# A decoder layer on one core: the branch of the top-k selection asked for directly behind its searches, two query projections queued behind its flag, and the selection masks built one behind the other

## The chip, the core and the metric

The kernel runs on one core of one Trainium2 chip. A core has five engines that run side by side, each through its own list of instructions in order: PE (TensorE, matrix products and transposes), DVE (VectorE), ACT (ScalarE), POOL (GpSimd) and SP (here only a queue that starts DMA transfers). An engine waits for another by a semaphore. The metric is device time in microseconds (us) of one execution, and what is compared is the median of several runs. Matrix products here are 128 rows deep and write up to 512 columns into a PSUM bank.

## The reference

One layer of a hybrid decoder trunk on 1024 positions of 1024 channels. The part that matters here is the sparse attention: an indexer scores every earlier position for each query position, the 256 best are selected, and eight query heads attend to those alone.

```python
score = einsum('bth,bths->bts', w, relu(dots))          # the indexer, 128 query rows at a time
score = where(causal, score, -inf)
_, idx = top_k(score, 256)                              # 256 keys for each of the 1024 queries
kg, vg = k[idx], v[idx]                                 # two kv heads, eight query heads
logits = einsum('btkgd,btjkd->btkgj', qg, kg) * 64**-0.5
p = softmax(where(sel_ok, logits, -inf)); o = einsum('btkgj,btjkd->btkgd', p, vg)
```

The rest of the layer (adaptive norms, a spatial gating unit, output projection, and a feed-forward block of 4096 channels) stands around it and is not touched.

## The kernel before

The 1024 positions are cut into 8 blocks of 128 query rows, numbered 0 to 7; block b has 128(b+1) causal keys. Blocks 0 and 1 have no more than 256 keys, so nothing is selected there, and their mask is the causal one alone. For blocks 2 to 7 the kernel does not gather: it finds for each row the value of the 256th score and turns the scores into an additive mask `BI` (0 for a selected key, a huge negative number for others).

- **Search** (`select`, L602 to L628): for each block a bitwise search, on DVE (L585, L587, L589) or on ACT (L597), for the upper 16 bits of the threshold, then a shortcut for the lower 16 bits that works as long as at most 8 keys share the upper bits.
- **Branch** (`search_rest`, L630 to L642): DVE counts in `more` the blocks in which the shortcut did not do (L632), PE sums this over the partitions with a 1x1 product (L634, the *flag*), DVE turns the sum into an integer `rest` (L635), reads it into a register (L637) and branches (L638) over a second search of the lower bits. The branch stands in a critical section: the program is cut there into blocks of instructions, every engine has a jump to its next block at that place, and DVE waits in front of its own jump for what the other engines have ahead of theirs.
- **Mask** (`mask(b)`, L644 to L660): three instructions on one column (L648, L649, L651) build the threshold `tf`; then over the row of scores L654 (below the threshold, with a count), L655 (equal to it), L656 (a running sum of the equal ones), two one-column instructions (L657, L658), L659 (which equal ones are too many) and L660 (the mask into `BI`).
- **Query projections** (`q_proj`, L542 to L547): 24 products of 512 columns for a block (`proj`, L296 to L302), a copy by ACT (L546), the rotary embedding on POOL.
- **Attention** in 32 units (L689), four for each block, in the block order 0, 7, 1, 6, 5, 4, 3, 2. For each pair of units `q_stack` makes the left operand (transposes on PE, L319, a copy on ACT, L379, and the rest of its high and low split on DVE, L380). A unit takes the products with the keys (L704), adds `BI` and takes the maximum on DVE (L705), the exponential on ACT (L708), then transposes (L743), copies (L724) and products with the values (L729).

The order on each engine is made by a scheduler from priorities: a smaller number goes first, and `stage(n)` sets the counter to 100000 n. Searches have numbers from 400000 on, the q projections stand in stage 4, and attention in stage 6. `after(ins, prev)` (L82) asks that one instruction stand behind another in the order, without a semaphore. In the program before, `search_rest()` and `mask(7)` are called in the loop over units, at u == 3, and the other masks behind units 4, 6, 8, 9 and 10 (L801); the scheduler may pull a mask ahead, and it does.

Of the kernel before, what the change touches and what calls it, by code (L numbers as in the profile page):

```python
# [16 lines left out]
OP = mybir.AluOpType  # L17
# [11 lines left out]
BIG = float(2.0 ** 100)  # L29
# [8 lines left out]
def trunk(ctx, tc, x, c, positions, w_ada, b_ada, g_pre_mix, w_in, g_sgu_v, w_spatial, b_spatial,  # L38
          g_out_sgu, g_out_attn, w_out, g_post_mix, g_pre_ffn, w_ff1, w_ff2, g_post_ffn, out):
    nc = tc.nc  # L40
    V, A, G, T = nc.vector, nc.scalar, nc.gpsimd, nc.tensor
# [5 lines left out]
    def nm(s):  # L47
        uid[0] += 1
        return f"{s}_{uid[0]}"
# [32 lines left out]
    def after(ins, prev):  # L82
        if prev is not None:
            tc.add_manual_dep(ins.ins, prev.ins.name,
                              mybir.DependencyInfo(mybir.DependencyClass.NoSync, mybir.DependencyReason.DATA),
                              reason="in this order")
# [4 lines left out]
    ones = ct([P, 1], F32, "ones")  # L91
# [45 lines left out]
    for k in range(KD):  # L137
        load_ada(0, (k,))
        if k:
            dst, src, off, n = small.pop()  # L140
            nc.sync.dma_start(dst, rows(src, off, n))
    for i in range(4):
        load_x(i)
        if small:
            dst, src, off, n = small.pop()
# [149 lines left out]

    def proj(p, j, wt, n, ks=range(KD)):  # L296
        h, t = hT[j // 4], (j % 4) * P
        for k in ks:
            lh, ll = h[:, 0, k, t:t + P], h[:, 1, k, t:t + P]
            T.matmul(p[:, :n], lh, wt[k][:, 0, :n], start=k == 0, stop=False)  # L300
            T.matmul(p[:, :n], lh, wt[k][:, 1, :n], start=False, stop=False)  # L301
            T.matmul(p[:, :n], ll, wt[k][:, 0, :n], start=False, stop=k == KD - 1)  # L302

    def rope(t, j, nh, pool):

# [40 lines left out]
    for j in range(NB):  # L346
# [4 lines left out]
        if j < 4:  # L351
            p = p1[j]
            proj(p, j, wC1, 328, range(4, KD))
        else:
            p = p_mm()
# [172 lines left out]
    for cc in range(2):  # L528
        wt = w_chunk(w_in, [(0, C_U + 256 * cc, 256), (256, C_V + 256 * cc, 256)])
        for j in range(NB):  # L530
            p = p_mm()
# [6 lines left out]
    wQ = w_chunk(w_in, [(0, C_Q, 512)])  # L538
    QT = {}
    OB = (0, 7, 1, 6, 5, 4, 3, 2)  # L540

    def q_proj(b):  # L542
        p = p_mm()
        proj(p, b, wQ, 512)
        QT[b] = qp.tile([P, 512], F32, tag="q", name=nm("q"), bufs=8)
        A.activation(QT[b], p, AF.Copy)  # L546
        rope(QT[b], b, 8, qp)  # L547

    for b in OB:
        q_proj(b)  # L550
        if pend:
            last_gelu = gating(*pend.pop(0))
# [14 lines left out]
    more = ct([P, 7], F32, "more")  # L567
# [62 lines left out]
    def search_rest():  # L630

        V.tensor_scalar(more[:, :6], KDS, 8.0, None, op0=OP.is_gt, op1=OP.add, accum_out=more[:, 6:7])  # L632
        p = p_tr()
        T.matmul(p[:1, :1], more[:, 6:7], ones, start=True, stop=True)  # L634
        V.tensor_copy(rest, p[:1, :1])  # L635
        with tc.tile_critical():
            r = V.value_load(rest)  # L637
            with V.If(r > 0):  # L638
                for b in range(2, NB):
                    cnt, sg, kk, tf, kq, lf, top8, kd, th, lo, hi = ST[b]  # L640
                    search(BI[:, boff[b]:boff[b] + P * (b + 1)].bitcast(U16), 15, lf, cnt, kd, kk, V.drain)
                V.drain()  # L642

    def mask(b):  # L644
        n = P * (b + 1)
        cnt, sg, kk, tf, kq, lf, top8, kd, th, lo, hi = ST[b]
        sc = score(b)
        V.tensor_copy(lo, lf)  # L648
        V.scalar_tensor_tensor(th, hi, 16, lo, op0=OP.logical_shift_left, op1=OP.bitwise_or)  # L649

        V.tensor_tensor(tf, th.bitcast(F32), sg, op=OP.mult)  # L651
        lt = BI[:, boff[b]:boff[b] + n]
        eq = up.tile([P, 1024], BF, tag="uv", name=nm("eq"), bufs=2)[:, :n]
        V.tensor_scalar(lt, sc, tf, None, op0=OP.is_lt, op1=OP.add, accum_out=cnt)  # L654
        V.tensor_scalar(eq, sc, tf, BIG, op0=OP.is_equal, op1=OP.mult)  # L655
        V.tensor_tensor_scan(sc, eq, eq, 0.0, op0=OP.add, op1=OP.max)  # L656
        V.tensor_scalar(cnt, cnt, float(TOPK - n), BIG, op0=OP.add, op1=OP.mult)  # L657
        V.tensor_tensor(cnt, cnt, sc[:, n - 1:n], op=OP.add)  # L658
        V.scalar_tensor_tensor(eq, sc, cnt, eq, op0=OP.is_gt, op1=OP.mult)  # L659
        V.scalar_tensor_tensor(lt, lt, -BIG, eq, op0=OP.mult, op1=OP.subtract)  # L660

    for b, pri in PRI:
        tc.cur_priority = pri
        select(b)


    stage(6)
# [135 lines left out]
    logits(0)  # L803
    stack_for(2)
    for u, (b, grp, pair) in enumerate(units):
        if u == 3:
            search_rest()
            mask(7)
        if u + 1 < len(units):
            logits(u + 1)  # L810
        values(u)
        if u in MASKS:
            mask(MASKS[u])
        if u == 12:
            u_stack.close()
            sc_stack.close()
            o_stack, op_ = push("op")
        stack_for(u + 3)
        if u % 4 == 2:
            finish_a(b)  # L820
        if u in (24, 28):
            ada_use(u // 4 - 4)
        if u in (20, 24, 28):
            ADA[u // 4 - 3] = ada_sum(u // 4 - 3)
        if u % 4 == 0 and u:
            finish(OB[u // 4 - 1])
        if u == 14:
            WO[0] = w_chunk(w_out, [(0, 0, 512)], gout, tile_of=wo_tile)
        if u >= 19 and u % 2:
            oproj0(OB[(u - 19) // 2])  # L830
# [71 lines left out]
    for j in range(NB):  # L902
# [4 lines left out]
        p = p_mm()  # L907
# [358 lines left out]
```

## Time and profile before

| what | before |
|---|---|
| median of 3 runs | 1272.2 us (1265.81 to 1272.71) |
| profiled execution, its own time | 1273.95 us |
| span of its instructions | 1272.2 us |
| PE busy in the span | 92% |
| DVE, ACT, POOL busy | 70%, 51%, 16% |
| mean granted TensorE clock | 0.959 of full |

Over the whole span PE is the engine that is always busy, so what matters is where it is not. The page cuts the span into 40 slices of 31.8 us and gives the busy tenths of each engine and the granted clock; the slices in which PE shows a low digit are the place to look at. Below that, three views are used: the busy times of each engine in chosen stretches, the list of who waited for whom, and the list of instructions in order of time. In the last one a row has the start in us, the duration in us, the engine, the line, the operation, out<-in, the shape, how many were merged, and in brackets the idle time before it and what ended it.

### The profile page before, as it was taken

What the parts mean: (1) busy time and instruction counts of PE and PEld (TensorE: products, weight loads), DVE (VectorE), ACT (ScalarE), POOL (GpSimd) and SP (SyncE); (2) the same over time, 40 slices, a digit from 0 to 9 for tenths busy, and PEclk for the clock granted to TensorE, in tenths of its full rate; (3) what the DMA queues carried; (4) which work ended last, traced back from release to release, by engine and by line L of the source; (5) the groups of instructions that cost most, each with busy time, mean ns of one, the idle gap of its engine ahead of it and who ended that gap; (6) DMA issues with size and microseconds to landing.
All of it is one profiled execution on the core that took longest, in us unless ns stands there. A gap on an engine that the chain in (4) does not pass through costs nothing.

```text
span 1272.2 us, 16825 instructions
## 1 busy us (share of the span) xinstructions
PE 1171.3 (92%) x5785; PEld 987.3 (78%) x5785; DVE 891.8 (70%) x1894; ACT 644.5 (51%) x1306; POOL 206.8 (16%) x280
## 2 busy tenths in 40 slices
PE   4889888889749999999889999999999899999997
PEld 4877677668639999878767878888888788888886
DVE  6833999987297656646898776556537846776668
ACT  4544557452327855545634555555544454445442
POOL 3675614132200000003630000000000000000001
PEclk9899999899759999989979999999999999999999
DMA  9420202010002124436404854344359355633335
GB/s 336 147 79 30 71 13 83 13 50 13 10 0 59 34 88 176 179 106 242 163 33 147 284 165 159 135 154 164 133 195 373 121 167 172 215 100 100 99 89 210
DMA packets 80240, 162.42 MB, mean 128 GB/s; under 512 B 7724, under 2 KB 32920, under 8 KB 80152
## 3 DMA queue, kind: packets, MB, share of 16 engines
q1 hardware_dynamic: 80136, 161.33, 37.7%
q8 instruction: 45, 0.74, 0.2%
q14 instruction: 43, 0.35, 0.1%
q10 hardware_dynamic: 16, 0.00, 0.0%
HBM read 119.36 MB, written 41.94 MB: 127 GB/s over the span
## 4 chain that ended last, share of the span: by engine, by line
PE 51%; DVE 12%; issue 4%; DMA 3%; ACT 1%; POOL 1%; SPq 0%; DVEq 0%; POOLq 0%; ACTq 0%
PE tr L1146 8%; PE lg L1146 8%; PE mm L1146 5%; PE mm L729 3%; PE lg L963 2%; PE lg L964 2%; PE lg L965 2%; DVE w L853 2%; PE tr L963 2%; PE tr L964 2%; PE tr L965 2%; PE tr L743 2%; PE lg L704 2%; PE mm L781 1%; PE mm L963 1%
## 5 line engine op out<-in xcount | busy, mean ns | idle before, releaser
L852 ACT ACTIVATE w<-rx 128x512 fp32r<-128x512 f32 x112 | 70.6, 630 | 148.5 <-PE lg L1146 61.2
L1146 PE MATMUL tr<-w,w 128*128 128x512 f32 x504 | 134.0, 391 | 3.8 <-DVE w L853 3.8
L1146 PE MATMUL lg<-w,w 128*128 128x512 f32 x504 | 133.7, 391 | 0.0
L300 PE MATMUL mm<-w,hT 128*128 128x512 f32 (+1 forms) x288 | 115.3, 401 | 9.8 <-ACT hT L293 3.8
L853 DVE TENSOR_TENSOR w<-rx,w 128x512 fp32r<-128x512 f32 x112 | 77.3, 690 | 58.9 <-ACT w L852 58.6
L1146 PEld LDWEIGHTS tr<-w,w 128*128 128x128 f32 x504 | 95.2, 189 | 24.0 <-DVE w L853 4.2
L302 PE MATMUL mm<-w,hT 128*128 128x512 f32 (+1 forms) x288 | 112.5, 391 | 0.9 <-POOL hT L294 0.9
L301 PE MATMUL mm<-w,hT 128*128 128x512 f32 (+1 forms) x288 | 112.5, 391 | 0.0
L1146 PEld LDWEIGHTS lg<-w,w 128*128 128x128 f32 x504 | 95.1, 189 | 19.8
L1182 POOL TENSOR_TENSOR rsf<-rsf,mhalf 128x1 f32<-128x1 f32 x8 | 6.0, 751 | 606.6 <-DVE rsf L1181 606.6
L1146 PE MATMUL mm<-w,w 128*128 128x512 f32 x336 | 94.3, 391 | 0.0
L729 PEld LDWEIGHTS mm<-VV,pT 128*128 128x128 f32 x576 | 74.3, 196 | 6.4 <-ACT pT L724 4.3
L729 PE MATMUL mm<-VV,pT 128*128 128x64 f32 x576 | 75.6, 275 | 2.9 <-ACT pT L724 2.9
L704 PE MATMUL lg<-KS,qs 128*128 128x512 f32 (+5 forms) x192 | 53.9, 394 | 24.2 <-DVE mxs L705 23.1
L300 PEld LDWEIGHTS mm<-w,hT 128*128 128x128 f32 x288 | 56.8, 197 | 21.5 <-ACT hT L293 4.0
L1146 PEld LDWEIGHTS mm<-w,w 128*128 128x128 f32 x336 | 63.2, 188 | 13.1
L853 DVE TENSOR_TENSOR w<-b,w 128x512 fp32r<-128x512 f32 x96 | 65.8, 686 | 4.5 <-ACT w L852 4.5
L302 PEld LDWEIGHTS mm<-w,hT 128*128 128x128 f32 x288 | 56.2, 195 | 10.9 <-POOL hT L294 1.2
L853 DVE TENSOR_TENSOR w<-s,w 128x512 fp32r<-128x512 f32 x56 | 38.2, 690 | 37.7 <-ACT w L852 37.7
L708 ACT ACTIVATE L<-L,mxs 128x128 f32<-128x128 f32 (+7 forms) x64 | 49.2, 770 | 30.0 <-DVE mxs L705 29.8
L301 PEld LDWEIGHTS mm<-w,hT 128*128 128x128 f32 x288 | 57.0, 198 | 8.9
L852 ACT ACTIVATE w<-b 128x512 fp32r<-128x512 f32 x96 | 59.3, 618 | 7.3 <-DMA b<-in_w_ff_dram 7.3
(356 smaller groups left out, 2969.5 us busy)
## 6 DMA issues: line engine op xcount, KB each, us to landing
rx<-x_scratch SPq DMA_DIRECT2D x56, 512.0 KB, 3.6
x_scratch<-d SPq DMA_DIRECT2D x108, 256.0 KB, 3.0
ada<-in_w_ada_dram SPq DMA_DIRECT2D x48, 512.0 KB, 6.0
raw<-in_w_ff_dram SPq DMA_DIRECT2D x32, 512.0 KB, 4.0
b<-in_w_ff_dram SPq DMA_DIRECT2D x32, 512.0 KB, 4.5
x<-in_x_dram SPq DMA_DIRECT2D x16, 512.0 KB, 5.6
raw<-in_w_in_dram SPq DMA_DIRECT2D x8, 512.0 KB, 3.5
raw<-in_w_in_dram SPq DMA_DIRECT2D x16, 256.0 KB, 2.8
```

The costliest lines, as they stand in the source:

```text
L300: T.matmul(p[:, :n], lh, wt[k][:, 0, :n], start=k == 0, stop=False)
L301: T.matmul(p[:, :n], lh, wt[k][:, 1, :n], start=False, stop=False)
L302: T.matmul(p[:, :n], ll, wt[k][:, 0, :n], start=False, stop=k == KD - 1)
L704: T.matmul(pl, QS[b, grp][:, q, h4 * P:(h4 + 1) * P], KS[:, grp, c0:c0 + cw], start=q == 0, stop=q == 1)
L708: ex = A.activation(L, L, AF.Exp, scale=-1.0, bias=top, accum_out=sms[:, b, h:h + 1])
L729: mm = T.matmul(po[:, o:o + 64], e[:, (si * 2 + h2) * P:(si * 2 + h2 + 1) * P], VV[:, s0 + si, grp], start=first, stop=pair == 1 and s0 + ...
L852: A.activation(hi, src, AF.Copy)
L853: eng.tensor_tensor(lo, src, hi.bitcast(F32), op=OP.subtract)
L963: ms.append(T.matmul(p, a[:, 0, k], b[:, 0, k], start=start and k == 0, stop=False, skip_group_check=more))
L964: ms.append(T.matmul(p, a[:, 0, k], b[:, 1, k], start=False, stop=False, skip_group_check=more))
L965: ms.append(T.matmul(p, a[:, 1, k], b[:, 0, k], start=False, stop=stop and k == 3, skip_group_check=more))
L1146: ms.append(T.matmul(p, x[:, qa, t * P:(t + 1) * P], y[:, qb], start=start and n == 0, stop=stop and n == 2, skip_group_check=more))
```

## The change

Three things are moved; no arithmetic is added or taken away.

1. `search_rest()` and `mask(7)` leave the loop over units and stand directly behind the searches, with priority 465000.
2. Of the eight query projections the last two (blocks 3 and 2) are made inside `search_rest`, behind the flag's product; `proj` returns its first product so that it can be ordered behind the flag.
3. Each mask's first instruction is ordered behind the last instruction of the mask before it.

```diff
     def proj(p, j, wt, n, ks=range(KD)):
+        first = None
         for k in ks:
-            T.matmul(p[:, :n], lh, wt[k][:, 0, :n], start=k == 0, stop=False)
+            mm = T.matmul(p[:, :n], lh, wt[k][:, 0, :n], start=k == 0, stop=False)
+            first = first or mm
...
+        return first
...
-    def q_proj(b):
+    def q_proj(b, behind=None):
         p = p_mm()
-        proj(p, b, wQ, 512)
+        after(proj(p, b, wQ, 512), behind)
...
-    for b in OB:
+    for b in OB[:6]:
         q_proj(b)
...
-        T.matmul(p[:1, :1], more[:, 6:7], ones, start=True, stop=True)
+        flag = T.matmul(p[:1, :1], more[:, 6:7], ones, start=True, stop=True)
         V.tensor_copy(rest, p[:1, :1])
+        for b in OB[6:]:
+            q_proj(b, flag)
         with tc.tile_critical():
...
+    masked = [None]
     def mask(b):
-        V.tensor_copy(lo, lf)
+        first = V.tensor_copy(lo, lf)
...
+        after(first, masked[0])
...
-        V.scalar_tensor_tensor(lt, lt, -BIG, eq, op0=OP.mult, op1=OP.subtract)
+        masked[0] = V.scalar_tensor_tensor(lt, lt, -BIG, eq, op0=OP.mult, op1=OP.subtract)
...
+    tc.cur_priority = 465000
+    search_rest()
+    mask(7)
...
     for u, (b, grp, pair) in enumerate(units):
-        if u == 3:
-            search_rest()
-            mask(7)
```

In the changed file the lines behind `proj` stand 3 lines lower, from `search_rest` on 3 to 12 lines lower. A row below names the line, the operation, out<-in with the numbers of the tiles, and the shape.

On PE, before, the flag (`tr_3247<-ones,more`) stands in the middle of the first attention units (`mm_3224` are products with the values for block 0, `tr_3239` and `tr_3872` transposes), with six transposes between it and PE's jump:

```order
L729 MATMUL mm_3224<-VV,pT_3228 128x64 x2
L683 MATMUL tr_3239<-ident,ya_3232 128x128 x4
L634 MATMUL tr_3247<-ones,more 1x1
L743 MATMUL tr_3872<-ident,L_3212 128x128
L743 MATMUL tr_3872<-ident,L_3218 128x128
L319 MATMUL tr_3884<-ident,qd_3882 128x128 x4
L1262 UNCONDITIONAL_BRANCH
L729 MATMUL mm_3224<-VV,pT_3875 128x64 x2
```

All eight projections lie far ahead of these rows.

On PE, in the changed program, the flag (`tr_3057`) stands behind the sixth query projection (`mm_2643`), and the seventh (`mm_3060`) stands behind it:

```order
L304 MATMUL mm_2643<-w_2458,hT_143 128x512
L637 MATMUL tr_3057<-ones,more 1x1 [waits DVE_49,PE_49]
L301 MATMUL mm_3060<-w_2431,hT_142 128x512 [waits Activation_49]
...
L301 MATMUL mm_3060<-w_2455,hT_142 128x512
L303 MATMUL mm_3060<-w_2455,hT_142 128x512
L1271 UNCONDITIONAL_BRANCH
L304 MATMUL mm_3060<-w_2455,hT_142 128x512
```

The flag moves ahead of all attention; between it and PE's jump there are now 20 of the 24 products of the seventh projection.

On DVE, before, behind the branch's NO_OP (the critical section's end) several masks are built at once, one instruction of each in turn (`self_2766` and `eq_3844` belong to block 7, the next lower numbers to block 6, 5, ...):

```order
L654 TENSOR_SCALAR BI,self_2766<-SC,self_2766 128x1024
L655 TENSOR_SCALAR eq_3844<-SC,self_2766 128x1024
L649 SCALAR_TENSOR_TENSOR seli_2757<-seli_2757 128x1
L654 TENSOR_SCALAR BI,self_2764<-SC,self_2764 128x896
L655 TENSOR_SCALAR eq_3959<-SC,self_2764 128x896
L654 TENSOR_SCALAR BI,self_2762<-SC,self_2762 128x768
L654 TENSOR_SCALAR BI,self_2760<-SC,self_2760 128x640
```

The six masks advance side by side, so that most neighbours in this list do not need each other's result.

On DVE, in the changed program, the branch follows the searches (`L631` is the last instruction of `select`) and the integer `rest`; its jump lists semaphores of every engine and queue:

```order
L631 ISA self_2690 128x1
L638 CAST rest<-tr_3057 1x1 [waits PE_49]
L641 NO_OP [waits DVE_49,Activation_49,Pool_49]
L1271 UNCONDITIONAL_BRANCH [waits DMAHW2_49,DMAHW1_49,DMAHW3_49,DMAHW0_49,DMAHW4_49,DVE_sequencer_49,DMAHW5_49,DVE_49,DMAHW6_49,PE_49,DMAHW7_49,Activation_49,Pool_49]
L642 TENSOR_LOAD rest
L643 COMPARE_AND_BRANCH
```

The branch's rows are the same as before; in front of them there is no attention any more.

On DVE, in the changed program, the mask of block 7 (`self_2700`, `eq_3720`) and nearly all of the one of block 6 (`self_2698`, `eq_3959`) stand ahead of the first unit's split `qs_3734`:

```order
L665 SCALAR_TENSOR_TENSOR SC<-eq_3720 128x1024
L667 TENSOR_TENSOR self_2700<-self_2700,SC 128x1
L668 SCALAR_TENSOR_TENSOR eq_3720<-SC,self_2700,eq_3720 128x1024
L669 SCALAR_TENSOR_TENSOR BI<-BI,eq_3720 128x1024
...
L665 SCALAR_TENSOR_TENSOR SC<-eq_3959 128x896
L667 TENSOR_TENSOR self_2698<-self_2698,SC 128x1
L668 SCALAR_TENSOR_TENSOR eq_3959<-SC,self_2698,eq_3959 128x896
L383 TENSOR_TENSOR qs_3734<-tr_3737,qs_3734 128x512
L669 SCALAR_TENSOR_TENSOR BI<-BI,eq_3959 128x896
L656 CAST seli_2697<-self_2696 128x1
L717 ISA L_3744,mxs<-lg_3745,BI 128x128
```

Before, this split stood directly behind the searches, and all four units of block 0 ahead of the branch. The masks of blocks 5 to 2 now stand between the instructions of the units of blocks 0 and 7, one mask at a time.

## Rows read from the trace of the kernel before

**Rows 1.** Page, 40 slices: busy tenths of PE, granted clock in tenths.

```profile
PE   4889888889749999999889999999999899999997
PEclk9899999899759999989979999999999999999999
```

**Rows 2.** Stretches: length, busy us of each engine, clock, DMA share, GB/s.

```profile
318.00:330.00 12.00, 11.20 (x53) 9.12 (x51) 1.14 (x7) 1.99 (x4) 3.90 (x10) 1.00 0.00 0
330.00:345.00 15.00, 13.29 (x64) 11.24 (x63) 5.20 (x24) 7.61 (x24) 2.88 (x7) 0.66 0.06 13
345.00:367.00 22.00, 0.00 (x0) 0.00 (x0) 18.61 (x51) 1.21 (x3) 2.53 (x2) 0.53 0.01 5
367.00:376.00 9.00, 7.81 (x22) 5.26 (x23) 9.00 (x21) 3.38 (x5) 0.00 (x0) 0.50 0.00 1
376.00:394.00 18.00, 18.00 (x141) 16.72 (x140) 18.00 (x42) 14.56 (x28) 0.76 (x1) 0.97 0.08 25
```

**Rows 3.** Waits, 318 to 400 us: us in total, times, longest.

```profile
PE lg L704 <- DVE mxs L705: 23.1, 2, 22.3
DVE seli L648 <- DVEq L636: 4.9, 1, 4.9
```

**Rows 4.** Instructions in order of time: DVE, end of the searches to the masks.

```profile
318.08 0.09 DVE L632 DVE_READ_ACCUMULATOR more<-kds 128x1 f32 x1
318.87 0.08 DVE L628 DVE_READ_ACCUMULATOR2_ANT self<- 128x1 f32 x1
329.77 0.69 DVE L380 TENSOR_TENSOR qs<-tr,qs 128x512 fp32r<-128x512 f32 x1 [10.83 <-ACT qs L379]
343.34 0.15 DVE L635 CAST rest<-tr 1x1 int32<-1x1 f32 x1 [3.08 <-PE tr L634]
348.39 0.34 DVE L648 CAST seli<-self 128x1 int32<-128x1 f32 x4 [4.91 <-DVEq L636]
```

**Rows 5.** Instructions in order of time: PE, last projection to block 7.

```profile
328.16 0.40 PE L302 MATMUL mm<-w,hT 128*128 128x512 f32 x1
338.85 2.91 PE L704 MATMUL lg<-KS,qs 128*128 128x512 f32 x6
343.63 0.63 PE L319 MATMUL tr<-ident,qd 128*128 128x128 f32 x4
367.19 2.07 PE L704 MATMUL lg<-KS,qs 128*128 128x512 f32 x4 [22.32 <-DVE mxs L705]
```

**Rows 6.** Instructions in order of time: ACT, the copy of the sixth projection.

```profile
317.71 0.60 ACT L546 ACTIVATE q<-mm 128x512 f32<-128x512 f32 x1 [4.84 <-PE mm L302]
```

**Rows 7.** Instructions in order of time: DVE, pieces of the masks.

```profile
350.25 0.16 DVE L649 SCALAR_TENSOR_TENSOR seli<-seli 128x1 int32<-128x1 int32 x1
350.32 1.28 DVE L654 TENSOR_SCALAR_CACHE_REDUCE BI<-SC,self 128x1024 bf16<-128x1024 f32 x1
351.51 0.76 DVE L655 TENSOR_SCALAR eq<-SC,self 128x1024 bf16<-128x1024 f32 x1
355.84 2.29 DVE L656 TENSOR_TENSOR_SCAN SC<-eq 128x1024 f32<-128x1024 bf16 x1
361.98 1.28 DVE L659 SCALAR_TENSOR_TENSOR eq<-SC,self,eq 128x1024 bf16<-128x1024 f32 x1
364.30 2.23 DVE L660 SCALAR_TENSOR_TENSOR BI<-BI,eq 128x1024 bf16<-128x1024 bf16 x2
```

**Rows 8.** Instructions in order of time: DVE, a search step, each waiting for the last.

```profile
301.65 0.21 DVE L587 TENSOR_SCALAR self<-self,kds 128x1 f32<-128x1 f32 x1
301.90 0.16 DVE L589 SCALAR_TENSOR_TENSOR self<-self 128x1 f32<-128x1 f32 x1
```

**Rows 9.** Instructions in order of time: DVE, first maximum of block 7, first of block 1.

```profile
366.44 0.69 DVE L705 CUSTOM_DVE_ANT_0 L<-lg,BI 128x512 f32<-128x512 f32 x1
394.76 0.42 DVE L705 CUSTOM_DVE_ANT_0 L<-lg,BI 128x256 f32<-128x256 f32 x1
```

**Rows 10.** Instructions in order of time: DVE, block 0's narrow maximum.

```profile
330.89 0.29 DVE L705 CUSTOM_DVE_ANT_0 L<-lg,BI 128x128 f32<-128x128 f32 x1 [0.42 <-PE lg L704]
```

## The prediction

> **What bounds the kernel now.** Read the page's slices first. PE is the busy engine, so the reader looks for the slices in which its digit is low: the eleventh and twelfth (318 to 382 us) have 7 and 4, and the clock digits there are 7 and 5, the longest trough in the page [rows 1]. Next the stretches [rows 2]: PE is full to about 330, half loaded in effect to 345 (busy 13.29 of 15, but at a mean clock of 0.66), does nothing at all from 345 to 367, runs at 0.50 (1.2 GHz, the lower of its two levels) to 376, and is full again from 376 on. DVE is the other way round: 1.14 of 12 us and 5.20 of 15 us busy while PE works, 18.61 of 22 while PE waits, and full from 367 to 394. So the two engines take turns here, and neither has to. The waits name the two links [rows 3]: PE stands 22.3 us in one piece for a maximum (L705), and DVE stands 4.9 us at the branch. The list in order of time shows why [rows 4, 5]: the searches end at 318.95, DVE then has nothing until 329.77, when PE has ended the eighth projection (328.56) and block 0's split arrives; the flag is read by DVE only at 343.34, behind block 0's units; the branch lets DVE go at 348.39; and block 7's first maximum, behind two whole masks and parts of the others, starts at 366.44 [rows 9]. What can be gained is the time between 318.95 and 343.34 in which the branch was not asked for, as far as PE has other work in it.
>
> **The change part by part.** I follow DVE in the changed order, with durations of before.
>
> *The flag.* `more` is ready at 318.17 [rows 4]. ACT's copy of the sixth projection starts at 317.71, so PE has ended it then and would have started the seventh at about 317.5 [rows 5, 6]; a product lasts 0.4 and overlaps its neighbours. The flag makes PE stand for about 0.7 us and be through at about 318.4. Queued behind it are the two projections and all of attention. They end about 0.9 us later than before, near 329.4; that costs nothing if DVE comes later still, which it does below.
>
> *The branch.* DVE reads the sum at about 319. But its jump waits for what PE has ahead of PE's own jump, and that is 20 products of the seventh projection. A projection takes 0.60 + 4.84 = 5.44 us [rows 6], so a product 0.227; the twentieth starts at 318.4 + 19 x 0.227 = 322.7 and ends at 323.1. Before, the last work of PE ahead of its jump ended at 343.63 + 0.63 = 344.26, and the masks began at 348.39, 4.13 later [rows 4, 5]. With the same 4.13 the masks begin at 327.2, which is 21.2 us earlier. If the wait of 4.9 [rows 3] counts from the read instead, whatever PE does, they begin at 324.0. The trace of before has the two causes 0.8 us apart and cannot tell them; I take 327.2, since the order lists PE among the semaphores of that jump.
>
> *The masks ahead of attention.* Block 7's: three of 0.16, then 1.28, 0.76, 2.29, two of 0.16, 1.28, and 8/15 of the merged 2.23, that is 1.19: 7.6 us [rows 7]. Block 6's up to L659: five of 0.16 and 7/8 of 5.61: 5.7. Together 13.3, so block 0's split can start at 340.5 instead of 329.77. PE, through with its projections at 329.4, has the first transposes and products and then stands about 10 us: this is the new wait, and it takes the place of the 22.3.
>
> In that sum I add nothing for the masks being one behind the other. A search step whose instructions need each other starts 0.25 us after one of 0.21, so 0.04 behind its end [rows 8]; an instruction that needs nothing starts 0.07 behind the start of one of 0.16 [rows 7], so 0.09 before its end. In a mask alone about six of ten are of the first kind and four of the second, which cancels. Interleaved, as before, nearly all are of the second kind, some 0.7 us less for a mask. *VectorE: DVE Perf Modes* of the Trainium skill, in "The DRAIN you can't avoid", has the pipe empty after each operation and a semaphore cost nothing, by which the one order would be worth as much as the other: if the masks went as fast as in the old order, block 0's split would come some 1.4 us earlier. The rows of this trace differ from that: the overlap is there when nothing is needed, and gone when something is.
>
> *Block 0's units to block 7.* Before, it took from the split at 329.77 to block 7's first products at 338.85 [rows 4, 5], and a pair of these takes a third of 2.91, about 1.0: 10.1 us, with the clock mostly at 0.50. DVE has in the same stretch, in the new order, the rest of mask 6 (1.1), mask 5 up to L659 (five of 0.16 and 3/4 of 5.61: 5.0), eight maxima of block 0 (at most 0.29 each, [rows 10]) and two splits (0.69). That is some 9 us, of which part falls into gaps of the chain; I add 0.9 to the chain and get block 7's first maximum at 340.5 + 11.0 = 351.5, against 366.44: 14.9 us earlier. Bounds: all of the 9 hidden, 350.6; a third of it exposed, 353.6.
>
> *Block 7's units.* Before, DVE was busy without a gap from there to block 1's first maximum at 394.76, 28.3 us [rows 2, 9]. In the new order most of mask 5 has left this stretch (3/4 of 0.76 + 2.29 + 1.28, 3.3 us) and the beginnings of masks 4, 3 and 2 have come in (L654 at 1.28 x (640 + 512 + 384)/1024 = 1.9, and nine of 0.16: 3.4). Four weight splits go behind it and the end of block 0 comes in, about as much. So the sum is unchanged, but DVE no longer has a backlog that keeps it fed: a maximum now waits in order for products of a PE at half clock. I take 1.6 us for that (bounds 0 and 6: sixteen wide maxima, each up to half its 0.69 late, is 5.5). Block 1's first maximum: 351.5 + 28.3 + 1.6 = 381.4, 13.4 earlier.
>
> *Behind that.* The output weights are split on ACT and DVE when the last mask has freed their space, which is now later with respect to the units, with two transfers behind them. I take 0.4 us (0 to 2). From there the order of every engine is the old one, so the gain stays: 13.0.
>
> The sum is made against the profiled execution's 1273.95: 1260.95. That execution lies 1.75 above the median of the runs shown, so against the median it is 1259.2. I predict 1259.
>
> **The rivals.**
>
> *The branch earlier.* If DVE doesn't wait for the 20 products, all behind it comes 3.2 us earlier: 1256. For it: only one wait is named at the branch [rows 3]. Against it: the jump's list of semaphores.
>
> *DVE paces block 7.* The 13.3 us of masks came first and emptied DVE's queue; if its order then fits the arrivals badly (each wide maximum waits and a mask's instruction waits behind it), the 1.6 goes to 6 and the weights cost 2: 13.0 - 4.4 - 1.6 = 7.0, so 1265. For it: DVE was full to 394 before, with no slack at all [rows 2]. Against it: the same sum of work.
>
> *PE stays at the lower level: slower.* PE will stand about 10 us in front of block 0's products, and its clock was 0.53 in the stretch in which it stood before, 0.50 behind it, and 0.97 only once it was full [rows 2]. *TensorE: Matmul & The Clock Gate* of the Trainium skill, Part 1, tells the same two levels, the lower one when idle, and this trace agrees with its 0.50. If PE's work now comes in pieces, so that the clock stays low for as much as the 18.0 us of work that it did at 0.97 from 376 to 394, this becomes 18.0 x 0.97/0.50 = 34.9, 16.9 longer: 1259.2 + 16.9 = 1276. It decides from about 13 us of full-clock work done at half clock. Against it: before, the clock came back although DVE set the pace.
>
> *Nothing changes.* The chain from the searches' end is as long whoever is asked first; then 1272. Against it: 10.8 us in which DVE had nothing [rows 4].
>
> **How the numbers follow.** Forecast 0.60, branch earlier 0.14, DVE paces 0.16, lower level 0.06, nothing 0.04. The forecast's own bounds (350.6 to 353.6, waits 0 to 6, weights 0 to 2) give 1256 to 1264. The range 1252 to 1268 takes in the earlier branch with its own spread and the DVE case, and leaves out the last two and a little at either end. A measurement of this kernel tells about 0.5% from no change, 6.4 us: faster means below 1265.8. The forecast, the earlier branch and about half of the DVE case are there: 0.81. The other half and the case of no change are within it, with most of the lower-level case: 0.15. Slower 0.04.
>
> **What would show it.** The read of the flag at about 319 and the first mask at 327 (324: the branch doesn't wait for the products). Block 0's split at 340 with PE's wait in front of it of about 10 us. Block 7's first maximum near 351, block 1's near 381. The clock back near full by 365. I am wrong if the masks begin later than 330, if the clock is still at 0.50 at 375, or if block 1's maximum comes less than 8 us earlier than it did.

## The result and the profile after

| what | before | after |
|---|---|---|
| median of the timed runs | 1271.49 us (8 runs) | 1258.42 us (8 runs, 1256.14 to 1263.57) |
| profiled execution, its own time | 1273.95 us | 1257.57 us |
| span; PE busy in it; mean clock | 1272.2; 92%; 0.959 | 1255.9; 93%; 0.969 |

The ratio is 0.991, with a 95% interval of 0.9886 to 0.9934: faster by 13.1 us. The page of the profile after answers to [rows 1]:

```profile
PE   4889899889698999999889999999999999999997
PEclk9889999899889999989989999999999999999999
```

The trough of two slices (PE busy 7 and 4 tenths, clock 7 and 5 tenths) is now one slice of 6 with a clock of 8. The stretches answer to [rows 2] (length, busy us of PE, PEld, DVE, ACT and POOL, clock, DMA share, GB/s):

```profile
318.00:330.00 12.00, 11.36 (x52) 9.10 (x51) 3.44 (x15) 1.20 (x2) 2.95 (x8) 1.00 0.00 1
330.00:340.00 10.00, 2.89 (x15) 1.94 (x13) 9.79 (x16) 2.96 (x4) 6.45 (x6) 0.69 0.00 0
340.00:350.00 10.00, 6.27 (x28) 5.76 (x28) 9.93 (x28) 3.74 (x15) 0.61 (x1) 0.50 0.01 2
350.00:360.00 10.00, 9.26 (x43) 7.20 (x41) 9.21 (x30) 4.71 (x12) 0.62 (x1) 0.78 0.07 26
360.00:370.00 10.00, 9.24 (x71) 8.42 (x71) 9.93 (x29) 7.35 (x15) 1.12 (x1) 1.00 0.01 2
380.00:394.00 14.00, 11.03 (x96) 10.32 (x96) 9.58 (x25) 12.02 (x28) 1.03 (x1) 1.00 0.33 104
```

DVE is nearly full from 330 on (9.2 to 9.9 of each 10 us up to 370); in the kernel before it was so from 348 [rows 2, 4]. PE is loaded again from 350, not 367. The waits, answering to [rows 3], show PE's wait of 22.3 us replaced by one of 8.4, and DVE's stand at the branch grown from 4.9 to 8.4:

```profile
DVE seli L656 <- DVEq L641: 8.4, 1, 8.4
PE lg L716 <- DVE qs L383: 8.4, 1, 8.4
```

DVE in order of time, answering to [rows 4, 9], from the sum of the flag to block 5's first maximum (128x384). Two rows of before have no counterpart in those groups and follow in the second fence: the first maxima of block 6 (128x448) and of block 5.

```profile
319.26 0.08 DVE L635 DVE_READ_ACCUMULATOR more<-kds 128x1 f32 x1
320.04 0.14 DVE L638 CAST rest<-tr 1x1 int32<-1x1 f32 x1
328.56 0.15 DVE L656 CAST seli<-self 128x1 int32<-128x1 f32 x1 [8.39 <-DVEq L641]
...
342.63 0.68 DVE L383 TENSOR_TENSOR qs<-tr,qs 128x512 fp32r<-128x512 f32 x1
...
353.04 0.69 DVE L717 CUSTOM_DVE_ANT_0 L<-lg,BI 128x512 f32<-128x512 f32 x1
...
380.84 0.41 DVE L717 CUSTOM_DVE_ANT_0 L<-lg,BI 128x256 f32<-128x256 f32 x1
...
383.42 1.42 DVE L225 SCALAR_TENSOR_TENSOR wo<-raw,cols,wo 128x512 fp32r<-128x512 f32 x2 [1.27 <-ACT wo L224]
...
389.51 1.76 DVE L225 SCALAR_TENSOR_TENSOR wo<-raw,cols,wo 128x512 fp32r<-128x512 f32 x2 [2.75 <-ACT wo L224]
...
399.93 0.62 DVE L717 CUSTOM_DVE_ANT_0 L<-lg,BI 128x448 f32<-128x448 f32 x1 [0.52 <-PE lg L716]
...
421.82 0.55 DVE L717 CUSTOM_DVE_ANT_0 L<-lg,BI 128x384 f32<-128x384 f32 x1
```

```profile
410.84 0.62 DVE L705 CUSTOM_DVE_ANT_0 L<-lg,BI 128x448 f32<-128x448 f32 x1 [0.51 <-PE lg L704]
...
432.72 0.56 DVE L705 CUSTOM_DVE_ANT_0 L<-lg,BI 128x384 f32<-128x384 f32 x1
```

PE in order of time, answering to [rows 5]: the flag, the twentieth product behind it, the first products for block 0, and a stand among block 1's units.

```profile
319.49 0.19 PE L637 MATMUL tr<-ones,more 128*1 128x1 f32 x2 [0.64 <-DVE more L635]
...
324.05 0.39 PE L303 MATMUL mm<-w,hT 128*128 128x512 f32 x1
...
343.36 0.90 PE L716 MATMUL lg<-KS,qs 128*128 128x128 f32 x3 [8.37 <-DVE qs L383]
...
385.49 0.66 PE L755 MATMUL tr<-ident,L 128*128 128x128 f32 x4 [1.33 <-DVE mT L699]
```

This execution reaches the flag's sum 1.18 us later than that of before (319.26 against 318.08), in a part that was not touched. So that executions can be compared, the table counts all places from that sum, each from its own trace (us): the first mask instruction, block 0's split, and the first maxima of blocks 7, 1, 6 and 5. The last column is the ratio of the time to that of the kernel before, each from runs of both made side by side. The kernels below the first two are those of the experiments.

| kernel | mask | split | 7 | 1 | 6 | 5 | ratio [interval] |
|---|---|---|---|---|---|---|---|
| before | 30.3 | 11.7 | 48.4 | 76.7 | 92.8 | 114.6 | 1 |
| after | 9.3 | 23.4 | 33.8 | 61.6 | 80.7 | 102.6 | 0.991 [0.9886, 0.9934] |
| e_call | 15.6 | 16.4 | 37.1 | 67.1 | 84.4 | 106.3 | 0.9952 [0.9934, 0.9969] |
| e_nochain | 9.3 | 25.1 | 37.0 | 65.5 | 81.8 | 103.7 | 0.9934 [0.9913, 0.9955] |
| e_chain | 30.4 | 11.7 | 39.4 | 65.7 | 85.0 | 111.9 | 0.998 [0.9967, 0.9993] |
| e_gate | 5.8 | 8.2 | 29.8 | 56.9 | 79.4 | 101.3 | 0.9867 [0.9844, 0.989] |
| e_m6 | 9.3 | 17.4 | 29.6 | 55.4 | 79.8 | 101.2 | 0.9936 [0.9916, 0.9956] |
| e_wo | 9.6 | 23.7 | 34.1 | 61.9 | 77.4 | 104.3 | 0.9922 [0.9902, 0.9942] |
| e_copy | 9.3 | 22.8 | 32.6 | 60.4 | 81.0 | 102.9 | 0.99 [0.9875, 0.9925] |
| e_gate_wo | 5.6 | 8.2 | 29.3 | 56.5 | 72.0 | 98.6 | 0.9872 [0.9851, 0.9893] |
| e_all | 5.9 | 8.6 | 28.2 | 54.0 | 69.3 | 96.1 | 0.9834 [0.9815, 0.9853] |

The lead of a kernel at a place is how much earlier it gets there than another, counted in this way. From before to after it is 21.0 us at the mask, 14.6 at block 7, 15.1 at block 1 and 12.1 at blocks 6 and 5. Behind block 5's first maximum the kernels do the same work, and the profiled executions of the table still take between 832.6 and 839.5 us for it: so 12.1 and the 13.1 of the medians can't be told apart, and the two profiled executions above are 17.5 us apart at their ends, counted so.

### The profile page after: what moved, and what is told of

Read it like the earlier page. It is cut to its first block, busy times and chain, and to the rows that moved or that the text cites. A ratio compares the mean times of both kernels' runs of the same rounds, so it can differ in the third digit from the quotient of the medians.

```text
span 1255.9 us, 16822 instructions
## 1 busy us (share of the span) xinstructions
PE 1166.5 (93%) x5785; PEld 982.6 (78%) x5785; DVE 892.9 (71%) x1894; ACT 645.1 (51%) x1306; POOL 209.9 (17%) x280
## 4 chain that ended last, share of the span: by engine, by line
PE 58%; DVE 9%; issue 3%; ACT 2%; DMA 1%; POOL 1%; SPq 0%; DVEq 0%; POOLq 0%; ACTq 0%
PE tr L1155 8%; PE lg L1155 8%; PE mm L1155 5%; PE mm L741 4%; PE lg L972 3%; PE lg L973 3%; PE lg L974 3%; PE tr L972 3%; PE tr L974 3%; PE tr L973 3%; PE mm L972 2%; PE mm L974 2%; PE mm L973 2%; PE lg L716 2%; PE tr L755 2%
## 5 line engine op out<-in xcount | busy, mean ns | idle before, releaser
L862 DVE TENSOR_TENSOR w<-rx,w 128x512 fp32r<-128x512 f32 x112 | 77.4, 691 | 56.5 <-ACT w L861 56.3
L1155 PEld LDWEIGHTS mm<-w,w 128*128 128x128 f32 x336 | 63.1, 188 | 13.1
```

What stands on the lines that cost most here:

```text
L862: eng.tensor_tensor(lo, src, hi.bitcast(F32), op=OP.subtract)
L1155: ms.append(T.matmul(p, x[:, qa, t * P:(t + 1) * P], y[:, qb], start=start and n == 0, stop=stop and n == 2, skip_group_check=more))
```

## The experiments

In the expectations "block 6's first maximum of 384 columns" means the first maximum that is 384 wide; it belongs to block 5 (block 6's are 448 wide).

**The call alone, and where the branch's wait ends (e_call, e_gate).** e_call undoes parts 2 and 3; e_gate puts the two projections behind PE's jump.

```diff
-    for b in OB[:6]:
+    for b in OB:
         q_proj(b)
...
-        for b in OB[6:]:
-            q_proj(b, flag)
...
-        after(first, masked[0])
```

> The branch is called early, but all eight query projections stand ahead of the flag and the masks go side by side as before. Theory (DVE's jump waits for all that PE has ahead of its own jump, and what counts is when the masks begin): the flag's product follows the eighth projection at about 329.5 us, four transposes behind it, so the masks begin about 6 us later than in the changed kernel (near 334 to 335 instead of 328.6) and block 7's first maximum moves by about the same: 1264 to 1265 us. Rival (the early call alone is what gains, since PE waits for the masks anyway): 1258 us, as the changed kernel. Second rival (side by side, block 7's mask ends later, so block 0's split waits for more): over 1268 us.

Measured: 1264.44 us, as in the theory. PE, then DVE, in order of time:

```profile
329.51 0.19 PE L637 MATMUL tr<-ones,more 128*1 128x1 f32 x2
329.63 0.66 PE L322 MATMUL tr<-ident,qd 128*128 128x128 f32 x4
```

```profile
329.74 0.15 DVE L638 CAST rest<-tr 1x1 int32<-1x1 f32 x1 [9.77 <-PE tr L637]
334.72 0.34 DVE L654 CAST seli<-self 128x1 int32<-128x1 f32 x4 [4.84 <-DVEq L639]
```

The masks begin 6.3 us later than in the changed kernel, block 1's first maximum is 5.5 later, and the time 6.0 (5.3 by the ratios). So the early call alone, without the held projections and without the order of the masks, brings about half of the gain. How the other half divides between those two parts is not shown (see e_nochain).

```diff
-        for b in OB[6:]:
-            q_proj(b, flag)
...
-    mask(7)
+    began = mask(7)          # mask returns its first instruction
+    for b in OB[6:]:
+        q_proj(b, began)
```

> The changed kernel with the two held projections ordered behind PE's jump: between the flag and the jump PE has four transposes in place of 20 products. Theory (DVE's jump waits for what PE has ahead of its own): the masks begin 4 us earlier, at 324 to 325 instead of 328.6 (counted on the changed kernel's own flag at 319.5), and all behind it moves by 3 to 4 us: about 1254 to 1255 us. Rival (the wait at the branch is a fixed time from the read of the flag): masks at 328.6 all the same, 1258 us. Second rival (the projections now compete with block 0's units at half clock, and PE ends them later than block 0's split): gain lost, 1258 us or more although the masks begin earlier.

Measured: 1254.21 us; the interval of its ratio just touches that of the changed kernel. The flag is at 319.99 here. PE, then DVE:

```profile
320.12 0.65 PE L322 MATMUL tr<-ident,qd 128*128 128x128 f32 x4
```

```profile
320.44 0.14 DVE L638 CAST rest<-tr 1x1 int32<-1x1 f32 x1
325.54 0.15 DVE L654 CAST seli<-self 128x1 int32<-128x1 f32 x1 [4.95 <-DVEq L639]
```

Counted from the flag's sum the masks begin 3.5 us earlier, so DVE's jump does wait for the seventh projection when that stands ahead of PE's jump. There is a shortest wait as well. The first mask instruction comes 4.90 us behind the end of the flag's read in the kernel before, 4.83 in e_call and 4.96 in e_gate. After the change it comes 8.38 behind it, and 4.12 behind the twentieth product's end (324.44); in e_nochain, e_m6, e_wo and e_copy, which keep the products there, that second distance is 4.14 to 4.36. As these rows read, there are two conditions, one from the read and one from the products, and the later one decides. In the kernel before, its 4.90 from the read and its 4.13 from PE's last work both fit, so that trace alone could not give the second one. One thing is not parted: e_gate moves the projection's copy and rotary embedding together with its products.

The lead at block 1's first maximum (4.7 us over the changed kernel) is down to 1.3 at block 5. The stretch 384 to 396 us, in the changed kernel, in e_gate, and in a second execution of e_gate:

```profile
384.00:396.00 12.00, 8.22 (x69) 7.40 (x68) 7.75 (x20) 9.24 (x23) 1.58 (x2) 1.00 0.47 154
```

```profile
384.00:396.00 12.00, 11.86 (x54) 11.03 (x54) 5.83 (x17) 6.96 (x17) 1.17 (x2) 0.50 0.31 111
```

```profile
384.00:396.00 12.00, 11.86 (x54) 11.01 (x53) 6.29 (x21) 7.47 (x19) 1.77 (x3) 0.50 0.24 88
```

> A second profile of the kernel with the projections behind PE's jump. In the first, TensorE's granted clock was 0.50 from about 384 to 398 us, among block 1's units, which the changed kernel's trace does not show, and the lead of 4.6 us at block 1's first maximum was 1.3 at block 6's. Theory (this fall of the clock belongs to the one execution, and it is what ate the lead): this time no fall there, or at another place, and block 6's first maximum of 384 columns at 97.5 to 99 us behind the flag's sum instead of 101.3. Rival (the fall belongs to the kernel's order of work): the same 0.50 in the same units, 101 us again. Second rival (the lead is lost to the splits of the output weights, whatever the clock): 101 us without a fall.

Measured: 0.50 in the same units, block 5 at 102.2 (a single execution of 1260.47 us). The theory that this fall was of one execution is wrong: it came in both, so it goes with this kernel's order. At half clock PE is busy 11.86 of 12 us; from block 1's to block 6's first maximum it takes 22.5 and 23.6 us, against 19.1 in the changed kernel.

**The masks one behind the other (e_nochain, e_chain, e_m6).**

```diff
-        after(first, masked[0])
```

> The changed kernel without the masks one behind the other: flag and held projections as in it, the first instructions of the masks free. Theory (the sum of DVE's work from the branch to block 1's first maximum is the bound, and the order of the masks in it changes only the 0.04 behind the end against 0.09 ahead of it, at most 1 to 2 us in all): masks begin at 328.6 as in the changed kernel, block 0's split comes later than 342.6, because pieces of the masks of blocks 5 to 2 stand ahead of it, but block 1's first maximum stays within 2 us of 380.8: 1257 to 1260 us. Rival (the early end of masks 7 and 6 is what matters, since PE waits for block 0's split): each us by which the split is later is lost, some 4 to 8 us: 1262 to 1266 us.

Measured: 1261.98 us. Block 0's split is 1.7 us later, block 1's first maximum 3.9, which is more than the theory allowed (2). But block 5 is only 1.2 later: in this order the weight splits stand ahead of block 1 instead of among its units. The times differ by 3.6 us (3.0 by the ratios), but the intervals overlap: what the order of the masks is worth is not shown more closely.

e_chain is the kernel before with part 3 alone (the lines of the change's diff that name `masked`).

> The kernel before with the third part alone: masks one behind the other, branch still behind block 0's units. Theory (DVE's sum from the branch to block 1's first maximum is the bound): block 7's first maximum comes about 9 us earlier, since only its own mask stands ahead of it, and PE's wait of 22.3 us shrinks to about 13, but the rest of the masks then stands between the maxima and block 1's first maximum stays at about 394: 1270 to 1272 us, no change. Rival (PE's wait is the bound, whatever DVE does): 22.3 less 9 remains, 1262 to 1264 us.

Measured: 1268.24 us, 2.9 less than the runs of the kernel before beside it (1271.1); the theory had no change. PE's waits from 318 to 400 us; a stretch in which masks stand; then the stretches from block 1's to block 6's and from there to block 5's first maximum:

```profile
PE lg L707 <- DVE mxs L708: 13.7, 2, 13.4
```

```profile
380.00:394.00 14.00, 12.67 (x113) 12.29 (x113) 13.82 (x38) 9.25 (x21) 1.19 (x1) 1.00 0.08 20
383.90:403.21 19.31, 16.66 (x124) 15.50 (x124) 18.82 (x57) 12.67 (x31) 2.35 (x3) 0.91 0.06 15
403.21:430.06 26.85, 23.51 (x170) 21.80 (x171) 17.81 (x51) 19.50 (x40) 1.77 (x3) 0.94 0.21 70
```

PE's longest wait shrinks by 8.9 us, and the first maxima of blocks 7 and 1 come 8.9 and 11.0 earlier, yet block 5's only 2.8 and the time 2.9. The theory had block 1's first maximum stay, and it did not. Of the 8.2 us that are lost again, 3.2 go between blocks 1 and 6 (19.3 us against 16.1 before), where DVE works on the late masks, busy 18.82 of 19.31. The other 5.0 go between blocks 6 and 5 (26.9 against 21.9), where DVE is not full: in this order the weight splits stand at its start, from 400.50 on ACT to 409.46 on DVE, nearly as in e_wo below. The clock fell in both stretches too; an estimate from the mean clocks of the two rows gives that 1.7 and 1.6 us at most. So DVE's masks, the place of the splits and the clock share the loss.

```diff
+        if b == 6:
+            after(first, narrow[0])      # block 0's last maximum
```

> The changed kernel with the mask of block 6 ordered behind the last maximum of block 0, so that only block 7's mask stands ahead of block 0's split. Theory (from the branch to block 1's first maximum DVE's sum is the bound, and PE's wait of 8.4 us for the split costs nothing by itself): the split comes about 5.5 us earlier, near 337, PE's wait shrinks to about 3, block 7's first maximum comes earlier, and block 1's first maximum stays within 1.5 us of 380.8; 1256.5 to 1259 us. Rival (PE's wait is what is lost): all of it moves 5 us, 1253 us.

Measured: 1262.06 us. The stretch 380 to 394 us (changed kernel: DVE 9.58):

```profile
380.00:394.00 14.00, 10.12 (x81) 8.95 (x79) 13.78 (x42) 10.17 (x26) 2.13 (x3) 1.00 0.00 1
```

The split came 6.0 us earlier and PE's wait fell to 4.8. Block 1's first maximum moved by 6.2, again more than the theory allowed, and block 5's by 1.3; no gain in time. The rival's 1253 us did not come: a shorter wait of PE was by itself worth nothing here. The theory needs another end, as I now read it: DVE's sum up to the last mask bounds, wherever block 1 stands in it. From block 1's to block 6's first maximum:

```profile
375.11:399.51 24.40, 20.07 (x147) 18.66 (x147) 22.15 (x63) 15.80 (x38) 2.13 (x3) 0.89 0.19 55
```

That is 5.3 us more than the 19.1 of the changed kernel, where DVE is busy 12.04 us. The clock can account for 2.7 of it at most (estimate: 24.40 us at 0.89).

> A second profile of the kernel with block 6's mask behind block 0. In the first, block 7's first maximum came 4.1 and block 1's 6.2 us earlier than in the changed kernel, but block 6's first maximum of 384 columns only 1.3, with DVE busy 13.78 of the 14 us from 380 to 394 and a clock of 0.50 from about 394 to 400 us. Theory (DVE's sum up to the last mask is the bound, and a mask put behind block 1's first maximum is paid there): DVE full from 380 to 394 again, and block 6's maximum at 100 to 102.5 us with or without the fall. Rival (only the clock ate the lead): without a fall, 97 to 99 us.

Measured: DVE busy 13.72 of 14 us, block 5 at 101.2, as in the theory. The clock fell again too (0.50 from 396 to 399 us), so this run does not part the two causes; only the estimate above says that the clock was not all of it.

**The weight splits (e_wo, e_gate_wo).**

```diff
-            A.activation(hi, r, AF.Copy, scale=scale)
+            after(A.activation(hi, r, AF.Copy, scale=scale), held[0])
...
         if u == 14:
+            held[0] = EX[12]       # first unit of block 6, its last exponential
```

> The changed kernel with the splits of the output weights held, in ACT's order, behind the first exponential unit of block 6, so that they no longer stand among block 1's units. Theory (in the changed kernel DVE stood 1.27 and 2.75 us for these splits at 383 and 390 us, with block 1's maxima queued behind them, and that is the 3 us by which the gain shrinks between block 1's first and second pair of units): block 6's first maximum of 384 columns comes about 3 us earlier than in the changed kernel (about 99.5 us behind the sum of the flag, instead of 102.6), the first maximum of block 1 stays; about 1255.5 us. Rival (the splits only fill time in which block 1's units wait for PE and ACT anyway): no change, 1258 us; then the 3 us belong to the chain of block 1's units.

Measured: 1260.94 us, no gain. Block 6's first maximum does come 3.3 us earlier, so the splits had cost about that among block 1's units. But from there to block 5 it takes 27.0 us instead of 21.9. ACT, then PE in order of time:

```profile
400.46 2.55 ACT L226 ACTIVATE wo<-raw,cols 128x512 fp32r<-128x512 f32 x4
...
402.91 0.58 ACT L384 ACTIVATE qs<-tr 128x512 fp32r<-128x512 f32 x1
```

```profile
403.54 1.04 PE L720 MATMUL lg<-KS,qs 128*128 128x448 f32 x3 [1.38 <-ACT qs L384]
```

Four splits in a row now hold up the copy for PE's next operand, PE stands 1.38 us, and the clock is 0.51 from 404 to 410:

```profile
404.00:410.00 6.00, 5.54 (x25) 4.86 (x23) 3.46 (x10) 4.94 (x11) 0.55 (x1) 0.51 0.56 175
```

> A second profile of the kernel with the weight splits held. In the first the clock fell to 0.50 from about 403 to 410 us, and block 6's first maximum of 384 columns stood 104.3 us behind the flag's sum, against 102.6 in the changed kernel and 99.5 expected. Theory (the fall is of the execution, and covered a gain of about 3 us): without a fall there, 100.5 to 102 us. Rival (no gain from the hold): 102 to 103 us without a fall; or the same fall and 104 us again, and then the fall belongs to the kernel.

Measured: 0.50 from 405 to 411, block 5 at 104.5. The fall came in both executions of this kernel as well, and the cost of the splits was moved, not hidden.

> The two changes together that looked best: projections behind PE's jump, and the splits of the output weights held behind block 6's first unit. In the first of them alone DVE stood 3.19 us at 385 us for those splits, and the gain that it had at block 1's first maximum (4.6 us, counted from the flag's sum) was down to 1.3 at block 6's first maximum of 384 columns. Theory (the two add up): that maximum at about 98 us behind the flag's sum, 1251 us. Rival (block 1's units are paced by PE, ACT and the copies in between): 1254 us, as without the hold.

Measured: 1253.62 us, as e_gate and as the rival. In the profiles block 5 comes 2.7 us earlier than in e_gate (98.6, near the theory's 98); the times do not tell that from nothing.

**DVE and POOL side by side (e_copy), and all together (e_all).**

```diff
-        G.tensor_copy(qd, qv[:, :, None, :].to_broadcast([P, 4, 2, 64]))
+        if act:                    # the first three pairs of units
+            A.activation(qd, qv[:, :, None, :].to_broadcast([P, 4, 2, 64]), AF.Copy)
+        else:
+            G.tensor_copy(qd, qv[:, :, None, :].to_broadcast([P, 4, 2, 64]))
```

> The changed kernel with the copies that make the left operands of the first three pairs of units (L379) on ACT instead of POOL. Theory (a POOL instruction that reads and writes SBUF and a DVE instruction beside it wait for each other: in the changed kernel POOL's copy took 2.53 us beside the running sum and 1.60 later instead of 0.61, and L667, L668, L669 and L657 of DVE took 0.87 us more than alone): with two copies gone from POOL beside masks 7 and 6, at least half of the 0.87 us goes, the two masks take 13.3 to 13.7 us from the branch to block 0's split instead of 14.07; what is left stands beside the rotary embedding, which stays on POOL. In time 0.4 to 0.8 us, 1257.5 us, too little to tell from no change. Rival (DVE's instructions are longer for another reason): 14.1 us again.

Measured: 1256.63 us, not told from the changed kernel. The two masks take 13.46 us (328.27 to 341.73) instead of 14.07, so most of the excess over the 13.3 us foreseen went. DVE and POOL of the changed kernel, in order of time:

```profile
331.13 2.29 DVE L665 TENSOR_TENSOR_SCAN SC<-eq 128x1024 f32<-128x1024 bf16 x1
333.46 0.38 DVE L667 TENSOR_TENSOR self<-self,SC 128x1 f32<-128x1 f32 x1
333.87 1.45 DVE L668 SCALAR_TENSOR_TENSOR eq<-SC,self,eq 128x1024 bf16<-128x1024 f32 x1
```

```profile
331.29 2.53 POOL L379 COPY qd<-q 128x512 f32<-128x512 f32 x1 [3.61 <-PE tr L322]
...
335.58 1.60 POOL L379 COPY qd<-q 128x512 f32<-128x512 f32 x1
```

POOL's copy (0.61 alone) starts 0.16 behind the running sum and ends 0.40 behind its end; DVE's next instruction (0.16 alone) then lasts to the end of the copy. With the copy gone the rotary embedding is in its place, L314 with 2.13 instead of 0.46, and DVE's L670, the same step, takes 0.23:

```profile
333.16 0.23 DVE L670 TENSOR_TENSOR self<-self,SC 128x1 f32<-128x1 f32 x1
```

```profile
331.25 2.13 POOL L314 TENSOR_TENSOR ra<-q,CS 128x128 f32<-128x128 f32 x1 [3.88 <-ACT q L552]
```

e_all is e_gate_wo with these copies on ACT.

> The three parts together: projections behind PE's jump, weight splits held, the first three copies for the left operands on ACT. Theory (each takes away a piece of DVE's work or of its wait ahead of the last mask; the copies 0.4 to 0.8 us, as at block 0's split in the run with the copies alone): 1252 to 1253.5 us, which can't be told from the 1253.6 without the copies, but not slower. Rival (copies on ACT come late for block 7's operand, behind ACT's exponentials): 1255 us or more.

Measured: 1251.77 us. The interval of its ratio lies wholly under that of the changed kernel, so this version beats that and the kernel before. The interval meets that of e_gate_wo, so what the copies add is not shown. The first maximum of block 6, then of block 5:

```profile
388.30 0.62 DVE L725 CUSTOM_DVE_ANT_0 L<-lg,BI 128x448 f32<-128x448 f32 x1 [0.53 <-PE lg L724]
...
415.08 0.55 DVE L725 CUSTOM_DVE_ANT_0 L<-lg,BI 128x384 f32<-128x384 f32 x1
```

Between them lie 26.8 us, as in e_wo: the splits are paid there again. The copies with the projections behind PE's jump, but without the hold, were not tried.

## Why the prediction was right

The forecast was 1259 us and the gain 13.0; measured 1258.42 and 13.1. The mechanism was right: the branch asked for early starts DVE's masks early, and PE's long wait goes with it. That the total agrees to a tenth is luck, as the terms show. Point by point, the predicted times moved by the 1.18 us of this execution:

- **The flag and the branch: right.** The read was foreseen at 320.2 and came at 320.04; the first mask at 328.4, and came at 328.56. The jump waits for the products: the rival without that wait is ruled out by the 8.39, and e_gate shows the wait shorter when the projection is behind the jump. What I could not see is that 4.13 behind PE's last work and 4.9 behind the read are two conditions. The 4.13 was a choice between two readings of one row, and that it was nearly exact is partly luck: in the kernel before the 4.9 alone would explain that row.
- **The masks: the term was 13.3 us, measured 14.07.** Not the order in a row was mis-sized, but POOL beside DVE was left out. e_copy gives 0.6 of the 0.8 back. *SBUF — State Buffer* of the Trainium skill, "Who interferes with whom", has a VectorE instruction with two SBUF inputs and a GpSimd instruction that reads SBUF contend for a shared port, which the first to issue keeps for its whole length; the rows above agree, POOL's copy ending 0.40 us behind the running sum. On the order in a row, the section of *VectorE: DVE Perf Modes* of the Trainium skill that the prediction names says besides that a next instruction that is not held starts earlier, so the overlap in the rows is no difference from it.
- **PE's new wait: right in place, 10 foreseen, 8.37 found.** The transposes and first products took some of the time.
- **Block 7's first maximum: 11.0 from the split, measured 10.41.** So it came at 353.04, with 352.7 foreseen. Lead 14.6, foreseen 14.9. The list of DVE's work for this stretch, given as some 9 us, adds up to 9.8; that moves only the later bound, by 0.3.
- **Block 7's units: 28.3 + 1.6, measured 27.80.** No wait was added; DVE was busy 9.93 of 10 us from 360 to 370. The lead at block 1 was 15.1, foreseen 13.4. The rival in which DVE's order fits the arrivals badly is out: its 6 us of waits did not come.
- **The weights: 0.4 us foreseen (0 to 2), about 3 measured**, outside its bounds. The lead fell from 15.1 to 12.1 between blocks 1 and 6, where DVE stood 1.27 and 2.75 us for them. e_wo took 3.3 out of that place, and the stretch from block 6 to block 5 became 5.1 longer.
- **The lower clock level.** It was back by 356 us, so that rival did not come about in the changed kernel. A later fall, of which the prediction says nothing, did come in other kernels: in e_gate, e_wo and e_m6 the clock falls again in the units of blocks 1 and 6.

So two terms erred in opposite directions (+2.1 from block 7's stretch, including the waits that did not come; -3 from the weights, against -0.4), and the total is nearer than its parts. The reading that carried it is that DVE's sum from the branch on bounds the stretch. From the first mask instruction to the end of the last mask DVE is busy 39.66 of 39.67 us before, 51.74 of 53.16 after, 50.65 of 51.55 in e_chain and 56.13 of 61.85 in e_m6, with other units among the masks in each; a shorter wait of PE brought 2.9 us in e_chain and nothing in e_m6. That fits the reading, and shows that its end is not block 1's first maximum. That its end is the last mask is argued, not shown, since the weight splits and the clock moved in both.

## What to carry to other kernels

When one engine's backlog bounds a stretch, a wait that shrinks on its neighbour may be worth little (8.9 us in e_chain, for 2.9 in time); measure the lead behind the point where the backlog ends, not at the first instruction that moved. DVE's jump waited here for a projection that stood ahead of PE's jump, and the masks began 3.5 us earlier with that projection behind it (e_gate). So try long independent work behind such a jump, not just behind the flag. And work that filled a gap which a change closes (here the weight splits) has to be given a new place in the sum.

## What the runs showed of the hardware that was not expected

- DVE and POOL lengthen each other, also where each works on its own tiles: POOL 2.53 instead of 0.61 us, DVE 0.38 instead of 0.16 and 1.45 instead of 1.28. Before the change it is in the trace too: a one-column instruction of POOL beside the running sum of [rows 7] takes 2.52 us, while the median of the eight with this output is 0.55:

```profile
355.95 2.52 POOL L99 TENSOR_TENSOR rsb<-rsb,mhalf 128x1 f32<-128x1 f32 x1 [10.94 <-DVE self L657]
```

- TensorE's clock fell to 0.50 for some 5 to 14 us at a place that came again in a second execution of the same kernel (e_gate, e_wo, e_m6), in the units of blocks 1 and 6. PE had stood 1.38 us just before in e_wo, and 1.22 us some 2 us before in e_gate; the changed kernel has a stand of 1.33 us at 385 and keeps 1.00. Falls in these units are also in the single profiles of e_chain, e_copy, e_gate_wo and e_all. What decides it stays open.
